# Hybrid decoder layer: the output projection as seven half-size products of sums

## The chip, the cores and the metric

The kernel runs on one core of one Trainium2 chip. The metric is the device time of one execution in microseconds (us). The engines in the text: PE (TensorE, matmul), DVE (VectorE), ACT (ScalarE), POOL (GpSimd), SP (SyncE, which issues most DMAs).

## The reference

One sequence of 512 rows, width 2048. The three mixers give `diff_out` (512x1024), `ssd_out` (512x512) and `xattn_out` (512x512); what follows them is what the change is about:

```python
diff_out = o.reshape(B, S, DIFF_WIDTH) * jax.nn.silu(dg)      # 8 heads of 128 columns
...
mixed = jnp.concatenate([diff_out, ssd_out, xattn_out], axis=-1)
return x + rms_norm(mixed @ w_out, post_norm_w)               # w_out is 2048 x 2048
```

All is float32.

## The kernel before

Every dense product is made of three matmuls (`mm3`, L94 to L97): each operand is split into a high part in the matmul's 32-bit format and a low part, and hi\*hi, hi\*lo and lo\*hi are added up in PSUM. The high part is a copy on ACT (L247 for weights), the low part a subtraction on DVE (`sub_hi`, L100). Weights come in chunks of 128x1024 (512 KB) through `fetch`, which keeps three chunks loaded (`raw`) and two split (`whi`, `wlo`).

In order of time: projections, SSD mixer, cross attention, then the eight heads of differential attention. The gate products `dg` (48 matmuls of 512 columns for each of 8 heads) run beside the last heads' attention: ACT takes the SiLU (L835) and POOL multiplies the head's output with it (L836). Each head's output `do` is normalized by `col_sums` (L154 to L163: squares on ACT, an addition on DVE at L159, a split, one matmul) and `neg2_rstd`. The activations stand transposed: 16 k tiles of 128 feature rows by 512 sequence columns, `do` 0 to 7, then `zs` and `xo` (the tiles that the SSD and the cross attention left).

The output projection splits these 16 k tiles (`mxh`, `mxl`, L851 and L100) and walks `OUT_BLOCKS`: blocks of 512, 512, 512, 256 and 256 output columns, for each 16 k tiles by 4 row tiles by 3 matmuls. The order of the k tiles starts with `zs` and `xo` (`KORDER_OUT`). A block's four PSUM banks are squared on ACT into `ssq` and multiplied with the norm's weights on DVE (`evac_out`, L861 and L863). The last block is done row tile by row tile, so that each row tile's norm, residual addition (L891) and store run while PE works on the next.

A scheduler with a model of time sets the order on each engine within what the code and the buffers allow; each engine then works strictly in that order.

Of the kernel before, what the change touches and what calls it, by code (L numbers as in the profile page):

```python
# [68 lines left out]
def hymba_kernel(ctx: ExitStack, tc: tile.TileContext, x, mem, positions, pre_norm_w, w_in,  # L69
# [24 lines left out]
    def mm3(ps, ah, al, bh, bl, start, stop):  # L94
        nc.tensor.matmul(ps, ah, bh, start=start, stop=False)  # L95
        nc.tensor.matmul(ps, ah, bl, start=False, stop=False)  # L96
        nc.tensor.matmul(ps, al, bh, start=False, stop=stop)  # L97
# [122 lines left out]
    def split_chunk():  # L220
# [6 lines left out]
        if i >= len(chunks) - 4:  # L227
            j = i - (len(chunks) - 4)
            his, los = [], []
            for e in range(2):  # L230
                hi = ft(slots_p, [P, 2, 256], f"s{KORDER_OUT[4 * j + e]}", f"lwh{j}{e}", dt=F32R)
                lo = ft(slots_p, [P, 2, 256], f"s{KORDER_OUT[4 * j + 2 + e]}", f"lwl{j}{e}",
                        dt=F32R)
                rv = raw[:, e * 512:(e + 1) * 512].rearrange("p (k c) -> p k c", k=2)
                nc.scalar.activation(hi, rv, AF.Copy)
                sub_hi(lo, rv, hi)
                his += [hi[:, 0], hi[:, 1]]
                los += [lo[:, 0], lo[:, 1]]
            pieces[i] = (his, los)
            return  # L240
        else:
            hi = ft(wpool, [P, CHUNK], "whi", f"whi{i}", dt=F32R)
            lo = ft(wpool, [P, CHUNK], "wlo", f"wlo{i}", dt=F32R)
# [490 lines left out]


# [85 lines left out]
    for p in range(4):  # L821
# [7 lines left out]
        for i in range(2):  # L829
            head(2 * p + i, q[i], k[i], v_pair[p])  # L830
    for p in range(4):
        for i in range(2):
            ps = dense_ws(hT, S, f"dg{p}{i}")
            gt = ft(ap, [P, S], "raw", f"dgate{p}{i}", 2)
            nc.scalar.activation(gt, ps, AF.Silu)  # L835
            nc.gpsimd.tensor_tensor(do[2 * p + i], do[2 * p + i], gt, ALU.mult)  # L836
        exp_table()
# [91 lines left out]
```

## Time and profile before

| what | value |
|---|---|
| median of 3 runs | 918.95 us (918.36 to 919.58) |
| the profiled execution, its own time | 918.23 us |
| its span in the trace | 916.5 us |
| granted PE clock, mean | 0.995 |
| busy shares PE / DVE / ACT / POOL | 98% / 57% / 46% / 13% |
| output projection, first to last `wo` matmul | 728.05 to 907.67 us |

The span is the time from the first to the last recorded instruction; the execution's own time is 1.73 us longer. A share is busy time over the span. Times in the text below that have two decimals are positions in this span or durations of single instructions.

### The profile page before, as it was taken

To read this page: it belongs to the slowest core of one execution; us is meant where nothing else is said; L and a number is where in the kernel's file an instruction comes from. 1 tells how busy PE (TensorE), PEld (TensorE's weight loads), DVE (VectorE), ACT (ScalarE), POOL (GpSimd) and SP (SyncE) were. 2 spreads that over 40 slices of the span, in tenths; PEclk is the share of its full clock that TensorE was granted. 3 is DMA by queue.
4 is the path that set the end of the run, shared out by engine and by line. 5 is a ranking of instruction groups with operands and counts; after the bars stand their busy time and mean duration, and the time that the engine had idled before them with its cause. 6 is when DMAs were issued, how large, how long until landed. Compare 5 with 4: busy or idle time off the path is not lost.

```text
span 916.5 us, 12561 instructions
## 1 busy us (share of the span) xinstructions
PE 898.5 (98%) x4794; PEld 767.4 (84%) x4794; DVE 519.7 (57%) x974; ACT 425.2 (46%) x705; POOL 123.4 (13%) x134
## 2 busy tenths in 40 slices
PE   7899999999999999999999999999999999999996
PEld 6799888888888888898899889888788878888896
DVE  5674545595575432485867678586755653232336
ACT  4653344455356642344554455454676733231331
POOL 2320000006000113320240122114111010000000
PEclk9999999999999999999999999999999999999998
DMA  6963332354352333442433343333233262322228
GB/s 224 351 165 85 85 84 69 91 149 115 93 133 74 93 93 104 115 104 73 112 95 89 93 109 81 99 93 103 70 92 92 69 241 95 102 92 92 93 70 275
DMA packets 137093, 104.42 MB, mean 114 GB/s; under 512 B 8693, under 2 KB 121026, under 8 KB 136394
## 3 DMA queue, kind: packets, MB, share of 16 engines
q1 hardware_dynamic: 136010, 103.11, 39.4%
q8 instruction: 37, 0.61, 0.3%
q0 software_dynamic: 1024, 0.53, 0.2%
...
## 4 chain that ended last, share of the span: by engine, by line
PE 90%; DMA 3%; ACT 2%; DVE 2%; SPq 1%; POOL 1%; issue 1%; DVEq 0%; POOLq 0%; ACTq 0%
PE wo L96 6%; PE wo L97 6%; PE wo L95 6%; PE v L97 3%; PE v L95 3%; PE v L96 3%; PE q L95 3%; PE q L96 3%; PE q L97 3%; PE xbc L96 3%; PE xbc L97 3%; PE xbc L95 3%; PE k L96 3%; PE k L95 3%; PE k L97 3%; PE dg L96 2%
## 5 line engine op out<-in xcount | busy, mean ns | idle before, releaser
L100 DVE TENSOR_TENSOR wlo<-raw,whi 128x1024 fp32r<-128x1024 f32 (+2 forms) x149 | 188.3, 1264 | 215.2 <-ACT whi L247 202.1
L247 ACT ACTIVATE whi<-raw 128x1024 fp32r<-128x1024 f32 (+1 forms) x132 | 139.7, 1059 | 210.4 <-PE wo L97 89.0
L96 PE MATMUL wo<-wlo,mxh 128*128 128x512 f32 (+1 forms) x256 | 93.3, 365 | 0.0
L97 PE MATMUL wo<-whi,mxl 128*128 128x512 f32 (+1 forms) x256 | 93.1, 364 | 0.0
L95 PE MATMUL wo<-whi,mxh 128*128 128x512 f32 (+1 forms) x256 | 81.8, 366 | 0.9 <-ACT dgate L835 0.9
L97 PE MATMUL v<-whi,hTl 128*128 128x256 f32 (+1 forms) x256 | 72.9, 286 | 0.0
L96 PE MATMUL v<-wlo,hTh 128*128 128x256 f32 (+1 forms) x256 | 72.8, 285 | 0.0
L95 PE MATMUL v<-whi,hTh 128*128 128x256 f32 (+1 forms) x256 | 72.5, 285 | 0.0
L792 ACT ACTIVATE p<-sc,nm 128x128 f32<-128x128 f32 (+3 forms) x64 | 33.3, 524 | 63.1 <-DVE nm L788 57.7
L95 PEld LDWEIGHTS wo<-whi,mxh 128*128 128x128 f32 x256 | 48.0, 188 | 9.8 <-ACT dgate L835 1.4
L96 PEld LDWEIGHTS wo<-wlo,mxh 128*128 128x128 f32 x256 | 48.2, 188 | 8.3
L97 PEld LDWEIGHTS wo<-whi,mxl 128*128 128x128 f32 x256 | 48.2, 188 | 8.0
L96 PE MATMUL k<-hTl,whi 128*128 128x512 f32 x128 | 50.9, 397 | 0.0
L97 PE MATMUL xbc<-hTh,wlo 128*128 128x512 f32 x128 | 50.7, 396 | 0.0
L95 PE MATMUL q<-hTh,whi 128*128 128x512 f32 x128 | 50.7, 396 | 0.0
L97 PE MATMUL dg<-hTh,wlo 128*128 128x512 f32 x128 | 50.7, 396 | 0.0
L96 PE MATMUL dg<-hTl,whi 128*128 128x512 f32 x128 | 50.6, 396 | 0.0
L96 PE MATMUL xbc<-hTl,whi 128*128 128x512 f32 x128 | 50.6, 395 | 0.0
L95 PE MATMUL dg<-hTh,whi 128*128 128x512 f32 x128 | 50.6, 395 | 0.0
L97 PE MATMUL k<-hTh,wlo 128*128 128x512 f32 x128 | 50.5, 395 | 0.0
L96 PE MATMUL q<-hTl,whi 128*128 128x512 f32 x128 | 50.4, 394 | 0.0
L97 PE MATMUL q<-hTh,wlo 128*128 128x512 f32 x128 | 50.4, 394 | 0.0
...
## 6 DMA issues: line engine op xcount, KB each, us to landing
...
```

What stands on the lines that cost most here:

```text
L95: nc.tensor.matmul(ps, ah, bh, start=start, stop=False)
L96: nc.tensor.matmul(ps, ah, bl, start=False, stop=False)
L97: nc.tensor.matmul(ps, al, bh, start=False, stop=stop)
L100: nc.vector.tensor_tensor(lo, src, hi.bitcast(F32), ALU.subtract)
L247: nc.scalar.activation(hi[:, :n], raw[:, :n], AF.Copy)
L792: nc.scalar.activation(pc[c][:, :w], sc[c][:, :w], AF.Exp, bias=nm[:, c:c + 1], scale=DSC, accum_out=ls[:, c:c + 1])
```

## The change

The output projection is done as Strassen's scheme in Winograd's form, one level deep. The 2048 inputs are halved in k (tiles `zs`, `xo` against tiles `do`), the 512 rows of a weight group's output in halves of 256, and the 2048 output columns go in four groups of 512, each halved into 256. Instead of eight block products of a group there are seven, each between a weight block or a sum of weight blocks (`U1` to `U4`) and an activation block or a sum of activation blocks (`N1`, `N2`, `T3`, `T4`). A product is four units of k; a unit is 12 matmuls of 128x256, so a group has 28 units and the projection 1,344 matmuls where there were 576 of 512 columns and 384 of 256.

- Weight blocks are loaded as 128x1024 tiles. In groups 0 to 2 POOL forms `U1` and `U3` (two additions of 128x1024 each, L957) and DVE `U2` and `U4`; in the last group DVE forms `U3`, POOL the others.
- Each unit's weights are split 512 columns at a time (`owh` on ACT, `owl` on DVE), three units ahead of the unit that is issued, in four buffers.
- Activation sums are formed in place on DVE (`sums_c`, 16 instructions of 256; `comb_d`, 8) and split (`cA`, `cB`, `cC`, 8 each of 512; `cD`, 8 of 256).
- The products are recombined on DVE (`T`, one operand in PSUM), squared on ACT and multiplied with the norm's weights on POOL in groups 0 to 2, on DVE in the last (`finish`).
- The SiLU of a gate is written back to PSUM, and the gate's multiplication is on DVE instead of POOL.
- The last two products of the last group run in row halves; the rows' norm, residual addition (now 8 instructions of 256 for each row tile) and store follow.

The diff, cut:

```diff
-    mixed = [None] * KT
-    for kt in KORDER_OUT:
-        src = (do + zs + xo)[kt]
-        mh = ft(big, [P, 512], "big", f"mxh{kt}", dt=F32R)
-        ml = ft(big, [P, 512], "big", f"mxl{kt}", dt=F32R)
-        nc.scalar.activation(mh, src, AF.Copy)
-        sub_hi(ml, src, mh)
-        mixed[kt] = (mh, ml)
...
-    tags = (("d", "d", "d", "tr"), ("sc", "sc", "sc", "av"))
-    for c in range(4):
-        col0, ncols = OUT_BLOCKS[c]
-        ps = dense_xs(mixed, [bank(tags[c % 2][t], f"wo{c}_{t}") for t in range(NT)], ncols,
-                      KORDER_OUT)
-        for t in range(NT):
-            evac_out(ps[t], t, c)
...
+    for a in zs + xo:
+        nc.vector.tensor_tensor(a[:, 256:], a[:, :256], a[:, 256:], ALU.subtract)
...
+            last_po = head(2 * p + i, q[i], k[i], v_pair[p])
+            if 2 * p + i < 7:
+                head_norm(2 * p + i, last_po, ap, "osq", "ory", "p1")
...
+    def gate_head(h, after=None):
+        ps = dense_ws(hT, S, f"dg{h}", after)
+        nc.scalar.activation(ps, ps, AF.Silu)
+        nc.vector.tensor_tensor(do[h], do[h], ps, ALU.mult)
...
+    def split_sum(j, kind, src, names):
+        hi = half_tile(f"c{kind}h{j}")
+        lo = half_tile(f"c{kind}l{j}")
+        nc.scalar.activation(hi, src, AF.Copy)
+        sub_hi(lo, src, hi)
+        for nm, cs in zip(names, (lsum, rsum)):
+            comb[j][nm] = (hi[:, cs], lo[:, cs])
...
+    def sums_c(j):
+
+        a, b = src1[j], do[j]
+        for cs, other in ((rsum, b[:, rsum]), (lsum, a[:, rsum])):
+            nc.vector.scalar_tensor_tensor(a[:, cs], other, -1.0, a[:, cs], ALU.mult,
+                                           ALU.subtract)
...
+    def comb_d(j):
+
+        a, b = src1[j], do[j]
+        nc.vector.scalar_tensor_tensor(b[:, lsum], a[:, rsum], -1.0, b[:, lsum],
+                                       ALU.mult, ALU.subtract)
+        both = half_tile(f"cD{j}")
+        nc.scalar.activation(both[:, lsum], b[:, lsum], AF.Copy)
+        sub_hi(both[:, rsum], b[:, lsum], both[:, lsum])
+        comb[j]["T4"] = (both[:, lsum], both[:, rsum])
...
+    plans = {(3, 0): [(comb_a, 4), (comb_a, 5)], (3, 1): [(comb_a, 6)], (4, 0): [(comb_a, 7)],
+             (6, 0): [(sums_c, 0), (sums_c, 1), (sums_c, 2), (comb_c, 0)],
+             (6, 1): [(sums_c, 3), (sums_c, 4), (comb_c, 1)],
+             (7, 0): [(sums_c, 5), (comb_c, 2)], (7, 1): [(sums_c, 6), (comb_c, 3)]}
+    head_norm(7, last_po, ep, "pw", "pw", "osp", 2, [(comb_a, j) for j in range(4)])
...
+    PROD = {1: ("A11", "B11"), 2: ("A12", "B21"), 3: ("U4", "B22"), 4: ("A22", "T4"),
+            5: ("U1", "N1"), 6: ("U2", "N2"), 7: ("U3", "T3")}
+    NG = D // 512
+    ORDER = [(1, 5, 7, 6, 2, 4, 3)] * (NG - 1) + [(1, 7, 6, 2, 4, 5, 3)]
+    seq = [(g, q, u) for g in range(NG) for q in ORDER[g] for u in range(4)]
...
+    def combine(g, eng, dst, a, b, at):
+        for u in range(2):
+            w = wt[g]
+            eng.tensor_tensor(w[at, u], w[a, u], w[b, u], ALU.add)
+            w[dst, u] = w[at, u]
+
+    def start_group(g):
+
+        if g == 0:
+            for nm in ("A11", "A21"):
+                load_block(0, nm)
+        load_block(g, "A22")
+        for u in range(2):
+            wt[g]["U1", u] = raw_tile(f"oU1_{g}{u}")
...
+        combine(g, nc.gpsimd, "U1", "A21", "A22", "U1")
+        if g < NG - 1:
+            combine(g, nc.gpsimd, "U3", "A11", "A21", "A21")
...
+        if g < NG - 1:
+            if q == 5:
+                combine(g, nc.vector, "U2", "U1", "A11", "U1")
+                load_block(g, "A12")
+            if q == 7:
+                load_block(g + 1, "A11")
+            if q == 6:
+                combine(g, nc.vector, "U4", "U2", "A12", "U1")
+            if q == 4:
+                load_block(g + 1, "A21")
+            if q == 3:
+                start_group(g + 1)
+            return
+        if q == 1:
+            combine(g, nc.vector, "U3", "A11", "A21", "A11")
+            combine(g, nc.gpsimd, "U2", "U3", "A22", "A21")
+        if q == 7:
+            load_block(g, "A12")
+        if q == 6:
+            combine(g, nc.gpsimd, "U4", "U2", "A12", "A21")
...
+    def split_product(n):
+        if n >= len(seq):
+            return
+        g, q, u = seq[n]
+        src = wt[g][PROD[q][0], u // 2][:, 512 * (u % 2):512 * (u % 2) + 512]
+        if n < len(seq) - 8:
+            hi, lo = (ft(ep, [P, 512], f"ow{x}", f"ow{x}{n}", 4, F32R) for x in "hl")
...
+        nc.scalar.activation(hi, src, AF.Copy)
+        sub_hi(lo, src, hi)
+        split[n] = [[t[:, 256 * k:256 * k + 256] for k in range(2)] for t in (hi, lo)]
...
+    def finish(g, r, c, ts=(0, 1)):
+        o = acc(g, r, c)
+        jk = ft(ep, [P, 256], "jk", f"jk{g}{r}{c}{ts[0]}", 2, BF16)
+        for t in ts:
+            nc.scalar.activation(jk, o[:, t], AF.Square, scale=1.0 / math.sqrt(D),
+                                 accum_out=ssq[:, 2 * c + t, 2 * g + r:2 * g + r + 1])
+        w = pws[g][:, r].unsqueeze(1).broadcast_to([P, len(ts), 256])
+        tt = slice(ts[0], ts[-1] + 1)
+        (nc.gpsimd if g < NG - 1 else nc.vector).tensor_tensor(o[:, tt], o[:, tt], w, ALU.mult)
...
+        for g in range(NG):
+            for r in range(2):
+                xs = xr[t, g // 2][:, (g % 2) * 512 + r * 256:(g % 2) * 512 + r * 256 + 256]
+                nc.vector.scalar_tensor_tensor(xs, oacc[g, r, t // 2][:, t % 2], y, xs,
+                                               ALU.mult, ALU.add)
...
+    def product(n, ps, ts=(0, 1)):
+        hi, lo = split[n]
+        g, q, u = seq[n]
+        for t in ts:
+            tsl = slice(t * P, (t + 1) * P)
+            for kk in range(2):
+                bh, bl = comb[2 * u + kk][PROD[q][1]]
+                last = mm3(ps[:, t], bh[:, tsl], bl[:, tsl], hi[kk], lo[kk],
+                    u == 0 and kk == 0 and t == ts[0], u == 3 and kk == 1 and t == ts[-1])
+        return last
...
+    rest = {2: [(comb_c, 4)], 3: [(comb_c, 5)], 4: [(comb_c, 6)], 5: [(comb_c, 7)],
+            6: [(comb_b, 0)], 7: [(comb_b, 1)], 8: [(comb_b, 2)], 9: [(comb_b, 3)],
+            10: [(comb_b, 4)], 11: [(comb_b, 5)], 12: [(comb_b, 6)], 13: [(comb_b, 7)],
+            14: [(comb_d, 0), (comb_d, 1)], 15: [(comb_d, 2), (comb_d, 3)],
+            16: [(comb_d, 4), (comb_d, 5)], 17: [(comb_d, 6), (comb_d, 7)]}
...
+        if q == 6 and g < NG - 1:
+            T(acc(g, 1, 1), acc(g, 0, 0), ps)
+            T(acc(g, 1, 0), acc(g, 1, 1), qps[g, 7])
+        elif q == 6:
+            T(acc(g, 0, 1), acc(g, 0, 0), ps)
+            T(acc(g, 1, 1), acc(g, 0, 1), qps[g, 7])
+        if q == 2:
+            if g < NG - 1:
+                T(acc(g, 0, 1), acc(g, 1, 1), qps[g, 5])
+                T(acc(g, 1, 1), acc(g, 1, 0), qps[g, 5])
+                finish(g, 1, 1)
+            T(acc(g, 0, 0), acc(g, 0, 0), ps)
+            finish(g, 0, 0)
+        if q == 4:
+            T(acc(g, 1, 0), acc(g, 1, int(g == NG - 1)), ps)
+            finish(g, 1, 0)
+        if q == 3:
+            T(acc(g, 0, 1), acc(g, 0, 1), ps)
+            finish(g, 0, 1)
...
+    for t in (0, 1):
+        load_rows(t)
+        write_rows(t)
+    g = NG - 1
+    N = len(seq)
+    for t in (0, 1):
+        load_rows(2 + t)
+        for q, n in ((5, N - 8), (3, N - 4)):
+            ps = qps2[q] if t else qps[g, q]
+            with tc.issue_after(last.ins):
+              for u in range(4):
+                last = product(n + u, ps, (t,))
+            for r in range(2):
+                if q == 5 or r == 0:
+                    T(acc(g, r, 1)[:, t], acc(g, r, 1)[:, t], ps[:, t])
+            finish(g, int(q == 5), 1, (t,))
+        write_rows(2 + t)
```

On DVE, at the end of the last head's attention (L159 is the addition in head 7's norm; `mxl` the splits of k tiles, `wlo` of weight chunks), before:

```order
L159 TENSOR_TENSOR osq_6214<-osq_6214,oup_6217 64x512
L100 TENSOR_TENSOR wlo_6687<-raw_6650,whi_6686 128x1024
L100 TENSOR_TENSOR mxl_6758<-z_2544,mxh_6757 128x512
L100 TENSOR_TENSOR osp_6218<-osq_6214,osp_6218 64x512
L100 TENSOR_TENSOR mxl_6762<-z_2607,mxh_6761 128x512
L100 TENSOR_TENSOR mxl_6766<-z_2698,mxh_6765 128x512
L100 TENSOR_TENSOR mxl_6770<-z_2761,mxh_6769 128x512
L100 TENSOR_TENSOR mxl_6774<-xo_1297,mxh_6773 128x512
L100 TENSOR_TENSOR wlo_6717<-raw_6684,whi_6716 128x1024
```

The same place in the change; `cAl` and `cCl` are splits of activation blocks, `owl` of a unit's weights, L868 is `sums_c`:

```order
L159 TENSOR_TENSOR osq_6357<-osq_6357,oup_6360 64x512
L100 TENSOR_TENSOR cAl_6369<-z_2544,cAh_6368 128x512
L100 TENSOR_TENSOR cAl_6373<-z_2607,cAh_6372 128x512
L868 SCALAR_TENSOR_TENSOR z_2544<-do_3605,z_2544 128x256
L100 TENSOR_TENSOR osp_6361<-osq_6357,osp_6361 64x512
L868 SCALAR_TENSOR_TENSOR z_2607<-do_3749,z_2607 128x256
L100 TENSOR_TENSOR owl_6829<-oA_00_6810,owh_6828 128x512
L868 SCALAR_TENSOR_TENSOR z_2544<-z_2544 128x256
L100 TENSOR_TENSOR owl_6833<-oA_00_6810,owh_6832 128x512
L868 SCALAR_TENSOR_TENSOR z_2607<-z_2607 128x256
L100 TENSOR_TENSOR owl_6837<-oA_01_6812,owh_6836 128x512
L100 TENSOR_TENSOR owl_6841<-oA_01_6812,owh_6840 128x512
```

The last two weight splits of the gates, which stood behind L159, stand before it, and all splits and sums that group 0 needs stand behind it: from there to the last `owl` of group 0 there are 64 instructions of 512 columns (28 `owl`, 8 each of `cA`, `cB`, `cC`, 5 recombinations, 7 of head 7's norm and gate), 24 scalar_tensor_tensors of 256 (16 `sums_c`, 8 `comb_d`), 8 `cD` splits and 4 multiplications of `pw` of 256, and 4 additions of 1024. On PE, 38 gate matmuls of 512 stand between head 7's last attention matmul and the first of group 0.

On POOL, from the first weight sum on, in the change (`oU`, `oA` are weight tiles of 1024; before, eight L836 multiplications and the one of `pw` stood here, and nothing behind them):

```order
L957 TENSOR_TENSOR oU_00_6822<-oA_00_6814,oA_00_6818 128x1024
L957 TENSOR_TENSOR oU_01_6823<-oA_01_6816,oA_01_6820 128x1024
L957 TENSOR_TENSOR oA_00_6814<-oA_00_6810,oA_00_6814 128x1024
L957 TENSOR_TENSOR oA_01_6816<-oA_01_6812,oA_01_6816 128x1024
L957 TENSOR_TENSOR oU_10_7361<-oA_10_7283,oA_10_7357 128x1024
L1032 TENSOR_TENSOR oacc_7182<-oacc_7182,pw_6913 128x512
L1032 TENSOR_TENSOR oacc_6917<-oacc_6917,pw_6913 128x512
L957 TENSOR_TENSOR oA_10_7283<-oA_10_7010,oA_10_7283 128x1024
```

POOL's work now goes on through the projection: four sums each for groups 0 to 2, six for the last, and four products with `pw` of 512 for each of the groups 0 to 2.

At the end of the program on DVE, before (the last row tile; `wo_3` is its last PSUM bank):

```order
L863 TENSOR_TENSOR oacc_6824<-wo_3_8079,pw 128x256
L885 TENSOR_REDUCE oss_8131<-ssq 128x1
L291 TENSOR_TENSOR ort_8134<-ors_8133 128x1
L292 SCALAR_TENSOR_TENSOR ort_8134<-oss_8131,ort_8134 128x1
L293 SCALAR_TENSOR_TENSOR ors_8133<-ort_8134,ors_8133 128x1
L891 SCALAR_TENSOR_TENSOR oacc_6824<-oacc_6824,ors_8133,xr_8077 128x256
L891 SCALAR_TENSOR_TENSOR oacc_6824<-oacc_6824,ors_8133,xr_8077 128x512 x3
L891 SCALAR_TENSOR_TENSOR oacc_6824<-oacc_6824,ors_8133,xr_8077 128x256
```

And in the change, from the last product's recombination (`oq33b`, behind the last matmul) on:

```order
L1098 TENSOR_TENSOR oacc_8668<-oacc_8668,oq33b 128x256
L272 TENSOR_TENSOR ort_8947<-ors_8946 128x1
L273 SCALAR_TENSOR_TENSOR ort_8947<-oss_8944,ort_8947 128x1
L1032 TENSOR_TENSOR oacc_8670<-oacc_8670,pw_8526 128x256
L274 SCALAR_TENSOR_TENSOR ors_8946<-ort_8947,ors_8946 128x1
L1032 TENSOR_TENSOR oacc_8668<-oacc_8668,pw_8526 128x256
L1043 TENSOR_REDUCE oss_9024<-ssq 128x1
L1050 SCALAR_TENSOR_TENSOR xr_8883<-oacc_7267,ors_8946,xr_8883 128x256
L1050 SCALAR_TENSOR_TENSOR xr_8883<-oacc_7182,ors_8946,xr_8883 128x256
L1050 SCALAR_TENSOR_TENSOR xr_8883<-oacc_7780,ors_8946,xr_8883 128x256
L1050 SCALAR_TENSOR_TENSOR xr_8883<-oacc_7711,ors_8946,xr_8883 128x256
L1050 SCALAR_TENSOR_TENSOR xr_8885<-oacc_8293,ors_8946,xr_8885 128x256
```

The eight residual additions of row tile 2 (L1050, with `ors_8946`) stand behind the last recombination and before row tile 3's own norm and its eight additions, which follow these rows. The 16 of row tiles 0 and 1 stand earlier.

## Rows read from the trace of the kernel before

**Rows 1.** The page: busy time and share of each engine; the chain that ended last.
```profile
PE 898.5 (98%) x4794; PEld 767.4 (84%) x4794; DVE 519.7 (57%) x974; ACT 425.2 (46%) x705; POOL 123.4 (13%) x134
...
PE 90%; DMA 3%; ACT 2%; DVE 2%; SPq 1%; POOL 1%; issue 1%; DVEq 0%; POOLq 0%; ACTq 0%
```

**Rows 2.** Windows: length, busy us per engine, granted PE clock, DMA share, GB/s.
```profile
core 0: us, PE busy (x) PEld busy (x) DVE busy (x) ACT busy (x) POOL busy (x), PEclk, DMA share, GB/s
...
728.00:862.00 134.00, 133.06 (x578) 107.97 (x577) 45.30 (x47) 41.40 (x58) 3.22 (x2) 1.00 0.35 121
862.00:907.50 45.50, 45.50 (x385) 45.46 (x383) 23.41 (x48) 12.92 (x35) 0.00 (x0) 1.00 0.42 131
907.50:916.50 9.00, 0.17 (x2) 0.00 (x0) 3.83 (x10) 0.97 (x4) 0.00 (x0) 0.71 0.73 275
```

**Rows 3.** Timeline of PE in the output projection: start, busy, operation.
```profile
728.05 0.84 PE L95 MATMUL wo<-whi,mxh 128*128 128x512 f32 x3
...
734.10 0.50 PE L95 MATMUL wo<-whi,mxh 128*128 128x512 f32 x1 [0.94 <-ACT dgate L835]
...
862.00 0.63 PE L95 MATMUL wo<-whi,mxh 128*128 128x256 f32 x4
...
907.39 0.28 PE L97 MATMUL wo<-lwh,mxl 128*128 128x256 f32 x1
```

**Rows 4.** Timeline of DVE at 732 us, back to back.
```profile
731.99 0.68 DVE L100 TENSOR_TENSOR mxl<-do,mxh 128x512 fp32r<-128x512 f32 x1
732.59 0.68 DVE L293 SCALAR_TENSOR_TENSOR ory<-osq,ory 128x512 f32<-128x512 f32 x1
733.19 1.22 DVE L100 TENSOR_TENSOR wlo<-raw,whi 128x1024 fp32r<-128x1024 f32 x1
734.32 0.75 DVE L818 SCALAR_TENSOR_TENSOR do<-do,subc,ory 128x512 f32<-128x512 f32 x1
```

**Rows 5.** Timeline of DVE, residual additions; the group of its 256-wide subtractions.
```profile
904.63 2.46 DVE L891 SCALAR_TENSOR_TENSOR oacc<-oacc,ors,xr 128x512 f32<-128x512 f32 x4
...
L100 DVE TENSOR_TENSOR vl<-v,vh 128x256 fp32r<-128x256 f32 x16 | 6.6, 419 | 1.3 <-ACT vh L428 1.3
```

**Rows 6.** Timeline of POOL at three places.
```profile
387.38 2.28 POOL L751 TENSOR_TENSOR sw_k<-sw_k,sinT 128x512 f32<-128x512 f32 x1
...
620.03 1.29 POOL L751 TENSOR_TENSOR sw_k<-sw_k,sinT 128x512 f32<-128x512 f32 x1
...
668.95 1.29 POOL L836 TENSOR_TENSOR do<-do,dgate 128x512 f32<-128x512 f32 x1 [10.60 <-ACT dgate L835]
```

**Rows 7.** Timeline of DVE at the same three places.
```profile
386.34 2.17 DVE L100 TENSOR_TENSOR wlo<-raw,whi 128x1024 fp32r<-128x1024 f32 x1 [3.55 <-ACT whi L247]
...
620.14 2.26 DVE L100 TENSOR_TENSOR wlo<-raw,whi 128x1024 fp32r<-128x1024 f32 x1 [1.95 <-ACT whi L247]
...
669.40 0.69 DVE L100 TENSOR_TENSOR aTl<-atr,aTh 128x512 fp32r<-128x512 f32 x1 [1.17 <-ACT aTh L803]
```

**Rows 8.** POOL's groups by shape: count, busy us, mean ns, idle before.
```profile
L836 POOL TENSOR_TENSOR do<-do,dgate 128x512 f32<-128x512 f32 x8 | 10.3, 1290 | 88.0 <-ACT dgate L835 74.2 <-DVE do L818 13.8
L629 POOL TENSOR_TENSOR conv<-conv,E 128x384 f32<-128x384 f32 x4 | 4.0, 1012 | 54.6 <-DVE E L628 43.0 <-DVE conv L622 11.6
```

**Rows 9.** Timelines of PE and DVE behind the last head's attention.
```profile
715.20 0.28 PE L97 MATMUL av<-aTh,vl 128*128 128x128 f32 x1
...
717.22 0.68 DVE L159 TENSOR_TENSOR osq<-osq,oup 64x512 f32<-64x512 f32 x1 [5.68 <-ACT oup L158]
```

**Rows 10.** Timelines of ACT and DVE behind the last matmul.
```profile
907.70 0.38 ACT L861 ACTIVATE jk<-wo 128x256 bf16<-128x256 f32 x1 [4.09 <-PE wo L97]
...
910.01 2.87 DVE L891 SCALAR_TENSOR_TENSOR oacc<-oacc,ors,xr 128x256 f32<-128x256 f32 x5 [0.17 <-DMA xr<-in_x_dram]
```

**Rows 11.** Timeline of ACT: copies of 512 columns back to back.
```profile
720.98 1.66 ACT L851 ACTIVATE mxh<-z 128x512 fp32r<-128x512 f32 x3
```

**Rows 12.** Windows early in the run, columns as in Rows 2.
```profile
0.00:10.00 10.00, 5.40 (x18) 4.18 (x19) 2.89 (x7) 3.60 (x6) 3.27 (x16) 1.00 0.73 231
20.00:30.00 10.00, 7.47 (x25) 5.13 (x24) 4.08 (x11) 7.33 (x12) 2.09 (x2) 0.86 0.85 319
```

More of the change, by code (lines that the diff above doesn't have):

```diff
@@ L96, in mm3 @@
         nc.tensor.matmul(ps, ah, bl, start=False, stop=False)
[L97 removed]
+        return nc.tensor.matmul(ps, al, bh, start=False, stop=stop)
     def sub_hi(lo, src, hi):
@@ L226, in split_chunk @@
         n = nkt * n1
[L227 to L243, printed above, removed]
+        hi = ft(wpool, [P, CHUNK], "whi", f"whi{i}", dt=F32R)
+        lo = ft(wpool, [P, CHUNK], "wlo", f"wlo{i}", dt=F32R)
         if i < N_POOL:
@@ L263, in dense_ws @@
             hi, lo = fetch()
+            if after:
+                after(ch)
             for kk in range(8):
@@ L829, in hymba_kernel @@
         for i in range(2):
[L830 to L837, printed above, removed]
+            last_po = head(2 * p + i, q[i], k[i], v_pair[p])
[5 more added lines that the diff above has]
+        nc.vector.tensor_tensor(do[h], do[h], ps, ALU.mult)
+    EARLY = 2
+    for h in range(EARLY):
+        gate_head(h)
     for _ in range(3):
@@ new lines, in hymba_kernel, with load_pw @@
+    for h in range(EARLY, 8):
+        gate_head(h, run_plan(h))
+    sums_c(7)
+    exp_table()
+    pws = {}
+    def load_pw(g):
+        pws[g] = ft(ep, [P, 2, 256], "pw", f"pw{g}", 2)
+        nc.sync.dma_start(pws[g].rearrange("p r c -> p (r c)"),
+                          post_norm_w[0, 512 * g:512 * g + 512].partition_broadcast(P))
+        for r in range(2):
+            nc.vector.tensor_scalar(pws[g][:, r], pws[g][:, r], (-0.5, 0.5)[r], None, ALU.mult)
+    ssq = const.tile([P, NT, 8], F32, name="ssq")
@@ new lines, in hymba_kernel, with raw_tile @@
+    PROD = {1: ("A11", "B11"), 2: ("A12", "B21"), 3: ("U4", "B22"), 4: ("A22", "T4"),
[3 more added lines that the diff above has]
+    seq = [(g, q, u) for g in range(NG) for q in ORDER[g] for u in range(4)]
+    wt = [{} for _ in range(NG)]
+    split = {}
+    nraw = [0]
+    def raw_tile(name):
+        nraw[0] += 1
+        at = (nraw[0] - 1) % 8
+        if at == 0:
+            return ft(ep, [P, 1024], "raw2", name, 1)
+        tag, bufs = (("raw", 3), ("whi", 2), ("wlo", 2))[(0, 0, 0, 1, 2, 1, 2)[at - 1]]
+        return ft(wpool, [P, CHUNK], tag, name, bufs)[:, :1024]
@@ L884, in hymba_kernel, with load_rows, write_rows @@
+    xr = {}
+    def load_rows(t):
+        for h in range(2):
+            xr[t, h] = raw_tile(f"xr{t}{h}")
+            nc.sync.dma_start(xr[t, h], x2[t * P:(t + 1) * P, h * 1024:(h + 1) * 1024])
+    def write_rows(t):
         ss = ft(small, [P, 1], "ss", f"oss{t}")
@@ new lines, in product @@
+    def product(n, ps, ts=(0, 1)):
+        hi, lo = split[n]
+        g, q, u = seq[n]
+        for t in ts:
[5 more added lines that the diff above has]
+        return last
+    V = nc.vector
+    start_group(0)
+    AHEAD = 3
+    for n in range(AHEAD):
+        split_product(n)
```

134 lines of the change are left out of this document (94 added, 40 removed).

## The prediction

> **What bounds the kernel now.** The page comes first: PE is busy 98% of the span and carries 90% of the chain that ended last, DVE is busy 57%, ACT 46%, POOL 13% [rows 1]. So matmul columns are what the time is made of. Those are averages, and the change touches one stage, so the second view is the windows of the output projection [rows 2]: from 728 to 907.5 us PE is busy 178.6 of 179.5 us at a granted clock of 1.00, DVE 68.7, ACT 54.3, POOL 3.2. PE has no slack there; DVE has 110 us of it, and POOL stands nearly still. The third view is PE's timeline in that stage [rows 3]. It gives the price of a matmul by starts: 576 of 512 columns between 728.05 and 862.00, less one idle gap of 0.94 us, are 0.231 us each; 383 of 256 columns between 862.00 and 907.39 are 0.1185 us each. Half the columns cost half the time, so cutting matmuls to 256 wide loses nothing by itself. Behind the last matmul (907.67) 8.8 us pass until the span ends at 916.5: PE works 0.17 us in that window [rows 2].
>
> **What the change should give PE.** 1,344 matmuls of 256 by 0.1185 us are 159.3 us; before, the stage took 907.67 less 728.05, 179.6 us. If PE were fed, 20.3 us would be gained. A unit is 12 matmuls, 1.42 us; a group of 28 units is 39.8 us. So the questions are whether DVE and POOL can feed units at that pace, and what the end costs.
>
> **DVE's prices.** Back to back, a DVE instruction of 512 columns starts 0.60 us after the one before it (731.99 to 732.59 to 733.19), one of 1024 takes 1.13 us (733.19 to 734.32) [rows 4]. A scalar_tensor_tensor of 256 is the difference of five such instructions (2.87 us, two of them of 256 and three of 512, [rows 10]) and four (2.46 us, [rows 5]): 0.41 us. A subtraction of 256 shows 0.42 us of its own [rows 5]; less the 0.08 us by which instructions in a row overlap (0.68 against 0.60) that is 0.34 us, which I take for the multiplications of `pw` too.
>
> **POOL's price, and what it does to DVE.** Before, POOL does no 1024-wide addition. Its 384-wide one takes 1.012 us, its 512-wide 1.290 us [rows 8]: 0.278 us for 128 columns, so 1.29 and four steps more are 2.40 us for 1024. The bounds are one of 512, 1.29, and two of them, 2.58. The Trainium skill, "GPSIMD Engine Reference", section 3.1 (elementwise, side by side), measures 4497 ns for an addition twice as long; half of that, an estimate, is 2.25 us, and the four additions of group 0 below would cost 0.6 us less by it.
>
> What matters more is that DVE and POOL stop each other. At 386.34 a 1024-wide subtraction on DVE takes 2.17 us instead of 1.22, and POOL's 512-wide product that begins at 387.38 takes 2.28 instead of 1.29; at 620.14 DVE's takes 2.26 beside one of POOL's of 1.29 [rows 6, 7]. The lengths fit one working at a time: at 620 POOL's first ends at 621.32, and 1.08 us more are DVE's own. At 669.40 DVE reads PSUM with one operand and takes 0.69 us, its own time, beside a POOL product that began at 668.95 [rows 6, 7]. So DVE's splits and sums, both operands in SBUF, wait out each POOL instruction; recombinations, with one operand in PSUM, don't. The upper bound of what a POOL instruction costs DVE is then its whole length; the lower is nothing, where DVE waits for something else anyway.
>
> **Group 0.** All activation sums and splits and the 28 weight splits of the group stand behind the L159 of head 7's norm. That instruction began 1.74 us after the end of head 7's last attention matmul (715.48 to 717.22, [rows 9]). In the change 38 gate matmuls of 0.231 us, 8.8 us, lie between that matmul and the first of group 0, so DVE starts its list 7.0 us ahead of the projection. The list: 64 of 512 by 0.60, 38.4 us; 24 of 256 by 0.41, 9.8; 12 by 0.34, 4.1; 4 of 1024 by 1.13, 4.5; together 56.8 us. POOL's four additions, 9.6 us, fall into the same stretch, for their tiles take the buffers that the last gate chunks leave; by the row at 620 I count them in full: 66.4 us. The last split is ready 59.4 us after the first matmul and group 0 ends one unit later, at 60.8, where PE alone would need 39.8. **That is 21 us of PE waiting for DVE, as much as the whole saving.** ACT is no bound there: its copies of 512 are 0.52 us (1.66 for three, [rows 11]), some 60 of them 31 us.
>
> **Groups 1 to 3.** PE needs 3 by 39.75, 119.3 us. DVE needs per group 35 to 36 of 512, 4 of 1024 and 2 of 256, 26.2 and 26.8 us, and POOL's four sums and four products (1.29 each) 14.8; summed, 41.0 and 41.6 against 39.75. In group 3 the splits of the last eight units stand early, so that 21.5 us of DVE and 19.6 of POOL (six sums, four products left from group 2), 41.1 us, must fit before unit 20, 28.4 us of PE. If every POOL instruction stops DVE, the excess is 1.3, 1.8 and 12.7, in all 15.8 us; the four split buffers lend 5.7 us (four units) against it. Bounds 0 and 15.8; I take 6, a little over half of the 10.1 left, since in these groups DVE also waits for buffers, and POOL's time then costs nothing.
>
> **The end.** Before, 2.34 us lie between the last matmul and the first residual addition (907.67 to 910.01), then 2.87 us of additions, then 3.6 us until the last store has landed [rows 10, 2]. In the change there is one more multiplication on the way (0.42, as the other 256-wide ones), and row tile 2's eight additions stand in DVE's queue between the last recombination and row tile 3's norm, whose own eight follow: 16 by 0.41, 6.6 us. 2.34 + 0.42 + 6.6 + 3.6 = 12.9. If row tile 2's eight were through in time it would be 9.7; at the 0.49 us that the busy time of one gives (0.41 and 0.08) 14.2.
>
> **What costs nothing.** The gates' multiplications move from POOL to DVE (8 by 0.60, one operand in PSUM), the first eight differences of 256 lie in cross attention: together some 8 us in stages where PE is busy and DVE, 57% over the span, is not; if that cover were gone, 8 us. The weights' DMA traffic is as before, at a DMA share of 0.35 to 0.42 [rows 2].
>
> **The sum.** 728.05 + 60.8 + 119.3 + 6 + 12.9 = 927.05 of span; with the 1.73 us that the profiled execution took beyond its span, **928.7 us**, against 918.23 for that execution and 918.95 for the median: 1.1% slower. What this kernel can tell from no change is about 0.2%, 1.8 us. Around it 922 to 935 for the likeliest case alone.
>
> **The rivals.**
> - *The saving and the bill cancel.* DVE pays in group 0 as above, but nothing stalls later and row tile 2's additions are through in time: 728.05 + 60.8 + 119.3 + 9.7 + 1.73 = 919.6. For it speaks that DVE waits for buffers in groups 1 and 2; against it group 3, whose list is longest. 0.09.
> - *The other side: POOL's sums cost DVE nothing.* If they fall where DVE waits for ACT's copies or a load, group 0 ends at 51.2 and later groups don't stall: 728.05 + 51.2 + 119.3 + 12.9 + 1.73 = 913.2, faster by 0.6%. It decides from the point where 11.6 of my 15.6 us of POOL's cost are gone (917.1). For it: POOL begins as soon as its tiles have landed, and DVE and ACT hand over to each other in small steps. Against it: DVE's own 56.8 us stand against 46.8 us (7.0 and 39.8) in which they would have to be done, so its list has hardly a gap to give. 0.16.
> - *Everything stalls.* All 15.8 us, and an end of 14.2: 939.9. 0.15.
> - *The clock.* In group 0 PE would be busy about two thirds. From 20 to 30 us, 75% busy, the granted clock was 0.86, though 1.00 in the first 10 us, 54% busy [rows 12]; at 907.5, with PE still, it is 0.71 over the window [rows 2]. The forecast keeps 1.00, by the first 10 us. If it fell to the lower level, 1.2 of 2.4 GHz, through group 0, a unit would take 2.84 us and the group 79.5 instead of 60.8: 947.4. The Trainium skill, "TensorE: Matmul & The Clock Gate", section "What's actually happening", says that the slow level is the default and activity releases it, which speaks for this rival. The trace agrees with it only in part, with 0.71 and 0.86 beside that 1.00. 0.07.
>
> That leaves 0.53 for the forecast. **Chances**: slower 0.53 + 0.15 + 0.07 = 0.75, the same 0.09, faster 0.16. The range: below 914 lies half of the faster case (0.08), above 938 the clock's (0.07) and part of the full stall (0.05), so 914 to 938 holds 8 in 10.
>
> **What the changed profile would show.** If right: in the first group (some 60 us from the first `oq` matmul) PE is busy two thirds, its idle time released by DVE's L100 of `owl` and the `c` tiles; DVE is near 100% there, with 512-wide splits of 3 us beside POOL's L957 of 2.4; the next groups take 40 to 44 us; the end behind the last matmul takes 13 us, with 16 L1050 in a row. Wrong, if the first group takes 40 to 50 us, if DVE shows idle gaps that ACT or a load ends while POOL works, if splits beside L957 keep their 0.6 us, or if row tile 2's additions lie before the last matmul.

## The result, and the profile after

The changed kernel takes 943.34 us (median of 4 runs, 942.87 to 944.16) against 919.03 for the kernel before: a ratio of 1.0266, 95% interval 1.0248 to 1.0284, slower by 2.7%. The forecast was 928.7 us, range 914 to 938: the direction was right, but 24.3 us were lost where 9.8 were forecast. The profiled execution took 943.54 us with a span of 941.8.

The page's first rows: busy time by engine, and the chain that ended last.

```profile
PE 893.7 (95%) x5178; PEld 780.5 (83%) x5178; DVE 638.9 (68%) x1157; ACT 466.3 (50%) x821; POOL 185.5 (20%) x155
...
PE 81%; DVE 10%; DMA 3%; issue 3%; POOL 1%; ACT 1%; SPq 0%; DVEq 0%; POOLq 0%; ACTq 0%
```

Beside [rows 1], PE gave up 9 points of the chain and DVE took 8. Where that is shows in windows, one for each of the four groups and one for the end (length, busy us per engine, granted clock, DMA share, GB/s):

```profile
729.38:789.27 59.89, 47.16 (x339) 44.83 (x338) 55.93 (x95) 33.02 (x66) 16.17 (x5) 0.89 0.24 75
789.27:835.96 46.69, 42.52 (x338) 41.43 (x337) 41.37 (x41) 22.11 (x50) 23.35 (x12) 0.96 0.33 102
835.96:880.44 44.48, 40.96 (x338) 39.94 (x337) 37.71 (x42) 21.59 (x45) 17.46 (x9) 1.00 0.31 101
880.44:929.50 49.06, 41.97 (x338) 40.22 (x336) 43.83 (x67) 19.84 (x46) 17.66 (x7) 1.00 0.41 138
929.50:941.80 12.30, 0.00 (x0) 0.00 (x0) 8.98 (x29) 1.90 (x8) 0.00 (x0) 0.64 0.56 220
```

Against the forecast's terms: the projection starts at 729.38 instead of 728.05 (1.3 us late), group 0 takes 59.9 us (forecast 60.8), groups 1 to 3 take 140.2 (forecast 119.3 and 6 of stalls), the end 12.3 (forecast 12.9). 1.3 − 0.9 + 14.9 − 0.6 are 14.7 us; 928.7 with them is 943.4, against the 943.5 of the profiled execution (the rest is rounding). One term is far off, that of groups 1 to 3: 20.9 us above PE's 119.3, where 6 were taken. PE's idle time ahead of the projection is 8.26 us before and after, so the late start is more busy time on PE, not a wait; which work it is was not looked into.

Group 0 is near the forecast in its length and in the engine that sets it. DVE's timeline, from head 7's norm to the last weight split of the group (start, busy; in brackets the idle time before an instruction and what ended it):

```profile
722.45 0.69 DVE L159 TENSOR_TENSOR osq<-osq,oup 64x512 f32<-64x512 f32 x1 [3.19 <-ACT oup L158]
...
733.13 0.41 DVE L868 SCALAR_TENSOR_TENSOR xo<-do,xo 128x256 f32<-128x256 f32 x1
733.46 0.41 DVE L868 SCALAR_TENSOR_TENSOR z<-z 128x256 f32<-128x256 f32 x1
733.80 0.68 DVE L100 TENSOR_TENSOR cAl<-xo,cAh 128x512 fp32r<-128x512 f32 x1
...
737.71 2.18 DVE L100 TENSOR_TENSOR owl<-oU,owh 128x512 fp32r<-128x512 f32 x1 [2.89 <-ACT owh L1011]
739.81 2.60 DVE L868 SCALAR_TENSOR_TENSOR z<-z 128x256 f32<-128x256 f32 x1
742.33 2.56 DVE L868 SCALAR_TENSOR_TENSOR xo<-xo 128x256 f32<-128x256 f32 x1
...
786.50 0.69 DVE L100 TENSOR_TENSOR owl<-oU,owh 128x512 fp32r<-128x512 f32 x1
```

The list runs from 722.45 to 787.19, where the group's 28th `owl` ends: 64.7 us; the forecast had 66.4. POOL's four sums cost DVE 2.9 us of waiting for the first one and 5.8 us in three held instructions, 8.7 of the 9.6 counted. The 24 scalar_tensor_tensors of 256 start 0.34 us apart where nothing holds them (733.13, 733.46, 733.80); the forecast took 0.41, which made the list 1.7 us too long.

PE did not wait for that last weight split, though. Its last gap in the group ends with an activation split, and the group ends 2.1 us behind the 28th `owl`, where the forecast had one unit, 1.4:

```profile
776.69 0.38 PE L97 MATMUL oq<-owh,cBl 128*128 128x256 f32 x1 [0.56 <-DVE cBl L100]
```

The end is as forecast: the eight additions of row tile 2 and those of row tile 3 stand behind the last matmul (929.5), one after the other.

```profile
931.62 3.25 DVE L1050 SCALAR_TENSOR_TENSOR xr<-oacc,ors,xr 128x256 f32<-128x256 f32 x8
...
935.36 3.26 DVE L1050 SCALAR_TENSOR_TENSOR xr<-oacc,ors,xr 128x256 f32<-128x256 f32 x8
```

Now the term that was off. DVE and POOL at the start of group 1:

```profile
790.08 3.46 DVE L100 TENSOR_TENSOR owl<-oA,owh 128x512 fp32r<-128x512 f32 x2
793.46 4.56 DVE L100 TENSOR_TENSOR owl<-oU,owh 128x512 fp32r<-128x512 f32 x2
798.06 3.28 DVE L957 TENSOR_TENSOR oU<-oU,oA 128x1024 f32<-128x1024 f32 x1
801.26 3.44 DVE L100 TENSOR_TENSOR owl<-oU,owh 128x512 fp32r<-128x512 f32 x2
804.63 2.85 DVE L100 TENSOR_TENSOR owl<-oA,owh 128x512 fp32r<-128x512 f32 x1
807.40 1.21 DVE L957 TENSOR_TENSOR oU<-oU,oA 128x1024 f32<-128x1024 f32 x1
```

```profile
788.25 3.02 POOL L957 TENSOR_TENSOR oU<-oA,oA 128x1024 f32<-128x1024 f32 x1 [43.64 <-DMA oA<-in_w_out_dram]
791.24 3.45 POOL L1032 TENSOR_TENSOR oacc<-oacc,pw 128x512 f32<-128x512 f32 x2
794.65 2.82 POOL L957 TENSOR_TENSOR oA<-oA,oA 128x1024 f32<-128x1024 f32 x1
797.44 2.82 POOL L957 TENSOR_TENSOR oU<-oA,oA 128x1024 f32<-128x1024 f32 x1
800.22 3.94 POOL L1032 TENSOR_TENSOR oacc<-oacc,pw 128x512 f32<-128x512 f32 x2
804.12 2.81 POOL L957 TENSOR_TENSOR oA<-oA,oA 128x1024 f32<-128x1024 f32 x1
```

POOL works through eight instructions without a gap from 788.25 to 806.93; such a stretch is called a burst below (the expectations say run). From 790.08 to 807.40 DVE gets eight done, one for each of POOL's; alone they would take 5.3 us (seven of 0.60, one of 1.13, [rows 4]). PE, which uses a split every 1.42 us, runs dry. The first and the last of its gaps that belong to a burst, in each of the groups 1 to 3:

```profile
798.08 0.38 PE L96 MATMUL oq<-owl,cAh 128*128 128x256 f32 x1 [1.09 <-DVE owl L100]
...
803.07 0.49 PE L96 MATMUL oq<-owl,cAh 128*128 128x256 f32 x1 [1.72 <-DVE owl L100]
...
839.28 0.39 PE L96 MATMUL oq<-owl,cAh 128*128 128x256 f32 x1 [0.17 <-DVE owl L100]
...
849.42 0.39 PE L96 MATMUL oq<-owl,cAh 128*128 128x256 f32 x1 [1.14 <-DVE owl L100]
...
885.92 0.39 PE L96 MATMUL oq<-owl,cAh 128*128 128x256 f32 x1 [2.32 <-DVE owl L100]
...
894.34 0.39 PE L96 MATMUL oq<-owl,cCh 128*128 128x256 f32 x1 [1.10 <-DVE owl L100]
```

POOL works from 788 to 807, from 833 to 848 and from 878 to 894 us, so these gaps lie in its bursts or within 2 us behind them. There are 13 gaps in the three groups, 14.6 us in all; DVE's `owl` ends 12 of them, and only two, 1.3 us together, lie elsewhere. The other 6.3 of the 20.9 us stand in PE's busy time (125.5 us against 119.3). A part of that is the clock: behind three gaps in group 1 the granted clock is 0.53 from 803 to 806 us. How much it cost there was not measured.

Behind the burst DVE has time, but can't use it; who waited for whom from 789 to 917.9 us (us in all, times, longest):

```profile
DVE owl L100 <- ACT owh L1011: 12.0, 22, 1.0
...
ACT owh L1011 <- PE oq L97: 38.9, 46, 2.3
```

DVE waits for the high part, and that for PE to free one of the four split buffers.

### The profile page after: what moved, and what is told of

It reads as the page before. It is cut to its first block, busy times and chain, and to the rows that moved or that the text cites. A ratio compares the mean times of both kernels' runs of the same rounds, so it can differ in the third digit from the quotient of the medians.

```text
span 941.8 us, 13732 instructions
## 1 busy us (share of the span) xinstructions
PE 893.7 (95%) x5178; PEld 780.5 (83%) x5178; DVE 638.9 (68%) x1157; ACT 466.3 (50%) x821; POOL 185.5 (20%) x155
## 3 DMA queue, kind: packets, MB, share of 16 engines
q0 software_dynamic: 1024, 0.53, 0.2%
## 4 chain that ended last, share of the span: by engine, by line
PE 81%; DVE 10%; DMA 3%; issue 3%; POOL 1%; ACT 1%; SPq 0%; DVEq 0%; POOLq 0%; ACTq 0%
PE oq L96 3%; DVE owl L100 3%; PE v L97 3%; PE v L95 3%; PE v L96 3%; PE oq L97 3%; PE q L96 3%; PE q L95 3%; PE q L97 3%; PE xbc L95 3%; PE xbc L96 3%; PE xbc L97 3%; PE oq L95 3%; PE k L96 3%; PE k L95 3%; PE k L97 3%
## 5 line engine op out<-in xcount | busy, mean ns | idle before, releaser
L100 DVE TENSOR_TENSOR wlo<-raw,whi 128x1024 fp32r<-128x1024 f32 (+2 forms) x121 | 150.9, 1247 | 124.4 <-ACT whi L226 110.5
L226 ACT ACTIVATE whi<-raw 128x1024 fp32r<-128x1024 f32 (+1 forms) x104 | 110.1, 1059 | 125.5 <-issue 29.0
L100 DVE TENSOR_TENSOR owl<-oA,owh 128x512 fp32r<-128x512 f32 x68 | 66.4, 990 | 7.3 <-ACT owh L1011 7.3
L776 ACT ACTIVATE p<-sc,nm 128x128 f32<-128x128 f32 (+3 forms) x64 | 33.4, 525 | 64.6 <-DVE nm L772 59.3
L1011 ACT ACTIVATE owh<-oA 128x512 fp32r<-128x512 f32 x68 | 42.4, 629 | 45.2 <-PE oq L97 34.4
L957 POOL TENSOR_TENSOR oU<-oA,oA 128x1024 f32<-128x1024 f32 x8 | 27.5, 3444 | 141.8 <-PE dg L96 89.8
L95 PE MATMUL k<-hTh,whi 128*128 128x512 f32 x128 | 50.4, 394 | 0.0
L95 PE MATMUL xbc<-hTh,whi 128*128 128x512 f32 x128 | 50.3, 393 | 0.0
L96 PEld LDWEIGHTS v<-wlo,hTh 128*128 128x128 f32 x256 | 48.4, 189 | 0.3
```

The lines of the kernel that those rows point to most:

```text
L100: nc.vector.tensor_tensor(lo, src, hi.bitcast(F32), ALU.subtract)
L226: nc.scalar.activation(hi[:, :n], raw[:, :n], AF.Copy)
L776: nc.scalar.activation(pc[c][:, :w], sc[c][:, :w], AF.Exp, bias=nm[:, c:c + 1], scale=DSC, accum_out=ls[:, c:c + 1])
L957: eng.tensor_tensor(w[at, u], w[a, u], w[b, u], ALU.add)
L1011: nc.scalar.activation(hi, src, AF.Copy)
```

## The experiments

Each ratio is to the kernel before, timed beside the run; its interval follows in brackets. Windows are of the groups 0, 1, 2, 3 in this order.

**All of POOL's work on DVE.**

```diff
-        combine(g, nc.gpsimd, "U1", "A21", "A22", "U1")
+        combine(g, nc.vector, "U1", "A21", "A22", "U1")
...
-        (nc.gpsimd if g < NG - 1 else nc.vector).tensor_tensor(o[:, tt], o[:, tt], w, ALU.mult)
+        nc.vector.tensor_tensor(o[:, tt], o[:, tt], w, ALU.mult)
```

(and the other three `combine` on POOL alike)

> All 18 weight sums and the 12 products with the norm's weights that POOL did in the projection are done by DVE; POOL does nothing there. Theory (POOL's instructions stop DVE in one run of eight at the start of each group, and the three units of lead can't bridge it): DVE's list per group is 26.5 + 4.5 + 2.4 = 33 us against 39.8 of PE, so groups 1 to 3 take 40 to 41 us each instead of 46.7, 44.5 and 49.1, and group 0, whose list is 56.8 + 4.5 us, takes about 56 instead of 59.9: 918 to 923 us. Rival (the waits in groups 1 to 3 are the hand-over from ACT to DVE to PE with a short lead, whoever forms the sums): DVE has 27 us more to do, 943 us or more.

926.04 us, ratio 1.0073 (1.0056 to 1.0091): 17 us less, with more work on DVE.

```profile
729.07:785.00 55.93, 46.57 (x339) 44.46 (x338) 54.42 (x99) 32.82 (x67) 0.00 (x0) 0.91 0.26 81
785.00:826.94 41.94, 40.17 (x337) 39.72 (x336) 37.24 (x53) 22.35 (x48) 0.00 (x0) 1.00 0.37 114
826.94:867.85 40.91, 40.27 (x339) 39.85 (x337) 34.18 (x51) 21.92 (x45) 0.00 (x0) 1.00 0.36 110
867.85:909.64 41.79, 40.84 (x338) 40.02 (x336) 38.53 (x74) 19.73 (x46) 0.00 (x0) 1.00 0.49 163
```

Groups 1 to 3 fall from 140.2 to 124.6 us, group 0 from 59.9 to 55.9. The median is 3 us above the expected range, and 5.3 us above PE's 119.3 stay; the hand-over rival, which needed 943 or more, is out.

**Only the products with the norm's weights on DVE** (the last line of that diff alone).

> Only the 12 products with the norm's weights move from POOL to DVE; the sums stay. Theory (each POOL instruction in the run of eight costs DVE its own length): three runs lose four products of 1.1 us of POOL's own time each, for 0.6 us on DVE outside the run: 930 to 938 us. Rival (hand-over): same or slower, 943 to 947.

944.06 us, 1.0274 (1.0257 to 1.0291): nothing gained; the expectation failed. The time lies in the rival's range, but the run above has ruled out the rival's cause. The moved product joins the queue that POOL's sums hold up, and waits out a sum itself:

```profile
834.03 2.90 DVE L1032 TENSOR_TENSOR oacc<-oacc,pw 128x512 f32<-128x512 f32 x1
```

**Only the sums on DVE** (the other half of the diff).

> Only the 18 sums move to DVE; the 12 products with the norm's weights stay on POOL. It is the other half of the run that moved the products alone and gained nothing. Theory (the sums are the cost, the products of 512 are not): 923 to 929 us, as with both on DVE. Rival (the two only pay together): 933 or more.

924.88 us, 1.0064 (1.0049 to 1.0079), groups 1 to 3 125.7 us. The sums are the whole of what POOL's work cost: with the products moved as well the kernel was no faster (926.04).

**No splits that wait for POOL's sums.**

```diff
-        src = wt[g][PROD[q][0], u // 2][:, 512 * (u % 2):512 * (u % 2) + 512]
+        nm = PROD[q][0]
+        if g < NG - 1 and q in (5, 7):
+            nm = "A22" if q == 5 else "A11"
+        src = wt[g][nm, u // 2][:, 512 * (u % 2):512 * (u % 2) + 512]
```

> POOL forms the same sums at the same size into the same tiles, but in groups 0 to 2 products 5 and 7 split an unsummed block instead (A22 for U1, A11 for U3), so that no split of these products waits for POOL; these products are not the ones that the output needs. It parts two ways in which POOL's sums can cost time: by stopping DVE, or by being late. Theory now (they stop DVE, and late in a group DVE idles because only four split buffers exist): groups 1 and 2 stay at 44 to 47 us each, the first wait of 3.4 us in group 0 goes, 936 to 943 us. Rival (the splits of products 5 and 7 wait for POOL's late sums): groups 1 and 2 take 40 to 42 us, 927 to 933.

948.81 us, 1.0323 (1.0307 to 1.0338), above both ranges. Groups 1 and 2 take 48.7 us each, and in them neither ACT nor DVE waits for POOL's result; all six gaps of PE are ended by DVE's `owl`. DVE, meanwhile, works back to back, and four splits that take 2.5 us alone take three times as long beside POOL:

```profile
794.88 7.36 DVE L100 TENSOR_TENSOR owl<-oA,owh 128x512 fp32r<-128x512 f32 x4
```

So in these groups the sums cost by stopping DVE, not by being late. In group 0, still 59.3 us, the wait did not go but moved: DVE's own sum for U2 now waits 2.28 us for POOL's U1. That the kernel became 5 us slower was not expected; in group 1 both of DVE's own sums for U2 now fall into POOL's burst, where one did, but whether that is the reason was not tested.

**Sums in four pieces.**

```diff
-            eng.tensor_tensor(w[at, u], w[a, u], w[b, u], ALU.add)
+            for i in range(4 if eng is nc.gpsimd else 1):
+                cs = slice(256 * i, 256 * i + 256) if eng is nc.gpsimd else slice(0, 1024)
+                eng.tensor_tensor(w[at, u][:, cs], w[a, u][:, cs], w[b, u][:, cs], ALU.add)
```

> The changed kernel with each of POOL's 18 sums of 128x1024 cut into four of 128x256; the same work stays on POOL. Theory (while POOL has work in a row, DVE gets one instruction in between two of POOL's, so what counts is the length of one POOL instruction): a split in the run waits 0.6 to 0.7 us instead of 2.2, DVE gives a split every 1.3 us where PE wants one every 1.4, and groups 1 to 3 take 41 to 44 us each: 928 to 936 us. Rival (what counts is the time that POOL holds DVE in all, which the cut doesn't lessen): 942 us or more.

946.34 us, 1.0295 (1.0281 to 1.0309): the theory in this form failed, and the time lies in the rival's range; groups 1 to 3 take 142.7 us. DVE's splits do get through faster (two in 1.96 us instead of 3.46), but POOL's second sum for U1 comes behind two products and half of U3, ACT can copy it only at 801.63 (800.29 in the change), and now DVE waits for that copy:

```profile
790.55 1.96 DVE L100 TENSOR_TENSOR owl<-oA,owh 128x512 fp32r<-128x512 f32 x2
...
802.29 2.91 DVE L100 TENSOR_TENSOR owl<-oU,owh 128x512 fp32r<-128x512 f32 x2 [5.81 <-ACT owh L1013]
```

So the length of one POOL instruction isn't what counts alone. That all the time for which POOL holds DVE comes back on one side or the other fits these rows, but is argued.

**Three split buffers instead of four.**

```diff
-            hi, lo = (ft(ep, [P, 512], f"ow{x}", f"ow{x}{n}", 4, F32R) for x in "hl")
+            hi, lo = (ft(ep, [P, 512], f"ow{x}", f"ow{x}{n}", 3, F32R) for x in "hl")
...
-    AHEAD = 3
+    AHEAD = 2
```

> The changed kernel with three split buffers instead of four, and splits two units ahead instead of three. Theory (POOL's sums stop DVE in one run per group, and only the lead of the split buffers, 1.4 us a unit, bridges it; DVE can't save up the idle time that it has later in the group): each of groups 1 to 3 loses 1 to 1.5 us more, 946 to 949 us. Rival (DVE's and POOL's work in a group, added up, is what a group takes): no change, 942 to 944.5.

951.74 us, 1.0356 (1.0341 to 1.0371): 8.4 us more, above the range; groups 61.9, 48.6, 45.2 and 52.0 us. The work of DVE and POOL in a group is the same as in the change, so it is not its sum that sets the time: the rival is out. The theory's sizes were not right either: groups 1 to 3 lost 2.0, 0.7 and 3.0 us, and group 0 lost 2.0, which it had not. More buffers were not tried, nor the same sums spread over the group.

**Group 0: the list.** The sums for T3 and N2 and their splits left out.

```diff
     def sums_c(j):
-
+        return
         a, b = src1[j], do[j]
...
-        split_sum(j, "C", src1[j], ("T3", "N2"))
+        ntile[0] += 2
+        comb[j]["T3"], comb[j]["N2"] = comb[j]["B11"], comb[j]["N1"]
```

> Leaves out the sums for the activation blocks T3 and N2 and their splits (products 7 and 6 use the blocks of products 1 and 5 instead, so these two products are not the ones that the output needs): 16 scalar_tensor_tensors of 256 and 8 splits of 512 less on DVE, 11.4 us, all in group 0's list; PE does as many matmuls. Theory (group 0 ends when DVE's list ends): group 0 about 48 to 50 us instead of 59.9, the kernel 931 to 935 us. Rival (POOL's late first sum and the lower clock set group 0's length, not the list): 939 to 944.

933.71 us, 1.0163 (1.0148 to 1.0179), group 0 50.9 us: 9.0 us less for 11.4 us of list (10.2 us by the 0.34 measured above).

**Group 0: the clock.**

```diff
+    FILL = {4: 16, 5: 6, 6: 16}
...
+        if n in FILL:
+            fill = bank("sc", f"fill{n}")
+            for _ in range(FILL[n]):
+                nc.tensor.matmul(fill, hA[0][:, :P], hA[0], start=True, stop=True)
```

> Adds 38 matmuls of 512 columns into a bank that nobody reads, at the places of group 0 where PE stood idle (before product 5 and before its third unit), 8.8 us of PE where 7.7 us were idle, so that the granted clock stays up. Theory (DVE's list ends group 0, so the lower clock was hidden behind it): granted clock near 1.00 in group 0, the group still 59 to 62 us, the kernel 942 to 946. Rival (the lower clock cost its own 5 to 7 us): 935 to 939.

943.96 us, 1.0271 (1.0256 to 1.0286). Group 0's clock rises from 0.89 to 0.97 and the group still takes 60.7 us. The same 10 us in the change and in this run:

```profile
738.00:748.00 10.00, 5.67 (x24) 5.01 (x24) 10.00 (x10) 4.65 (x9) 6.61 (x3) 0.52 0.01 2
...
738.00:748.00 10.00, 5.86 (x29) 4.97 (x30) 10.00 (x10) 4.72 (x10) 6.48 (x3) 0.85 0.01 2
```

The clock was 0.52 without the filling matmuls and 0.85 with them, and DVE was busy 10.00 of 10 us in both.

**Group 0 the plain way, all sums on DVE.** Eight block products, so that group 0 needs no sums; those of groups 1 to 3 are formed beside it (N1 as −N2 − B22, into the tiles of B12).

```diff
-    ORDER = [(1, 5, 7, 6, 2, 4, 3)] * (NG - 1) + [(1, 7, 6, 2, 4, 5, 3)]
+    ORDER = [(10, 11, 12, 13)] + [(1, 5, 7, 6, 2, 4, 3)] * (NG - 2) + [(1, 7, 6, 2, 4, 5, 3)]
...
+                    bh, bl = comb[2 * u + kk][("B11", "B12", "B21", "B22")[2 * k + c]]
+                    last = mm3(dps[r, c][:, t], bh[:, tsl], bl[:, tsl], hi[kk], lo[kk],
...
```

> All sums and products with the norm's weights on DVE, as in the run before that did this, and group 0 done in the plain way (eight block products, 384 matmuls of 256, splits of the unsummed blocks; the sums for groups 1 to 3 are formed beside it). Theory (group 0 is bound by DVE's list, which has to bring all activation sums and splits ahead of its matmuls): PE needs 45.5 us there, DVE's list of 48.5 us starts 7 us ahead, so group 0 takes 46 to 50 us instead of 55.9, the rest as in the run with all on DVE (124.6 and 12.4 us): 914 to 919 us. Rival (the plain group waits as long, since its second half needs splits that stand late in the list): 921 to 926.

916.11 us, 0.9971 (0.9960 to 0.9981): 0.3% faster than before. Group 0 takes 51.4 us, 1.4 above the expected range, of which 3.48 are one wait for ACT's `cBh`; groups 1 and 2 take 39.7 us each, PE's own time.

**The same with POOL's sums in pieces of 256** (`combine` on POOL as in the cut above).

> The kernel with the plain group 0, and POOL forms its sums again, in pieces of 128x256. Theory (short POOL instructions cost DVE little, and DVE is free of 4.5 us per group): the stalls at the start of groups 1 to 3 shrink, 1 to 5 us less than the kernel with all sums on DVE: 911 to 917 us. Rival (any POOL instruction costs DVE its length): 3 to 8 us more than that kernel.

923.77 us, 1.0055 (1.0041 to 1.0068): 7.7 us more than with the sums on DVE, the rival's upper end.

**The plain group with its lower blocks split first.**

```diff
+        rest[i] = [(comb_b, 2 * i), (comb_b, 2 * i + 1)]
+        rest[4 + i] = [(comb_c, 4 + i)]
```

(the last eight units' splits take the `ow` and `cmc` buffers, so that `big` is filled in this order)

> The kernel with the plain group 0 and all sums on DVE, with one change: the splits of the lower blocks (cB) come ahead of the sums for the later groups, which the plain group's second half waited 3.5 us for. Theory (that wait is on the path): group 0 takes 46 to 48 us instead of 51.4: 910 to 914 us. Rival (the wait moves to the cC and N1 splits that group 1 needs): 915 to 919.

910.03 us, 0.9899 (0.9882 to 0.9915), 1.0% faster than the kernel before. Group 0, 1 and the end:

```profile
729.29:774.95 45.66, 45.66 (x388) 45.62 (x387) 43.45 (x92) 26.10 (x60) 0.00 (x0) 1.00 0.32 102
774.95:814.25 39.30, 39.30 (x335) 39.30 (x334) 31.98 (x46) 21.52 (x45) 0.00 (x0) 1.00 0.37 115
...
895.95:908.40 12.45, 0.00 (x0) 0.00 (x0) 9.07 (x30) 1.90 (x8) 0.00 (x0) 0.71 0.57 220
```

PE has no idle time in the first two. Group 3, not shown, takes 42.0 us with one gap of 1.6 us. The end is as long as in the change.

**Its end without row tile 0's additions** (`if t > 0:` ahead of the scalar_tensor_tensor in `write_rows`).

> The fastest version so far, without the eight residual additions of row tile 0 (its rows are stored as the bare residual). Theory (DVE's queue is too long in the last products, so that row tile 2's eight additions fall behind the last matmul): the end behind the last matmul shrinks from 12.4 us by 2.5 to 3.3 us, 906.5 to 907.7. Rival (the end is the chain of the last row tile and the last store): 909.5 to 910.5.

910.07 us, 0.9904 (0.9887 to 0.9920): no change; the expectation failed, and the time lies in the rival's range. Row tile 2's additions now begin 0.4 us before the last matmul ends (896.2), but the order, planned anew, has the last recombination behind them:

```profile
895.81 3.26 DVE L1068 SCALAR_TENSOR_TENSOR xr<-oacc,ors,xr 128x256 f32<-128x256 f32 x8
898.99 0.42 DVE L1153 TENSOR_TENSOR oacc<-oacc,oq33b 128x256 f32<-128x256 f32 x1
```

So whether the end can be had in 9.7 us stays open; it was not settled by this run.

## Why the prediction was right in sign and wrong in size

- **What PE would gain** (20.3 us if fed): the price is right. In the fastest version groups 1 and 2 take 39.3 and 39.7 us at a clock of 1.00, against the forecast's 39.8. The whole 20.3 us were reached by no version: that one does group 0 the plain way, in 45.7 us, and group 3 in 42.0.
- **Group 0 is DVE's list**: right, by the list's length (64.7 us against 66.4), by DVE's busy time in the group (55.9 of 59.9 us) and by the run with a shorter list. That the group's time came within 0.9 us is in part luck: the sums of 256 were priced 1.7 us too high, and PE ended the group 0.7 us later behind the last weight split than forecast, a split for which it did not wait.
- **POOL's price, and that it stops DVE**: right in kind. The rows give 2.8 us for a sum in the burst; if 0.6 of it are the DVE instruction that was let pass, 2.2 are its own (an estimate), against the forecast's 2.40. The estimate from the Trainium skill, "GPSIMD Engine Reference", section 3.1, was 2.25, nearer to that.
- **The step that failed: "Groups 1 to 3", where DVE's and POOL's times were added up per group, set against 39.75 us, bounded at 15.8 and taken as 6.** The sum per group is not the measure. POOL's sums come in one burst around the start of a group, and during it DVE falls behind PE by more than the four split buffers hold; later in the group DVE is free but can't work ahead (12.0 us of waiting in 22 waits). So 20.9 us were lost where the excess over the group gave at most 15.8. That POOL's sums are the cause is shown by moving them alone to DVE (14.5 of the 20.9 us back, though DVE then has more to do) and by moving the products alone (nothing back). That they act by stopping DVE is shown, for groups 1 and 2, by the run in which neither ACT nor DVE waits for them there, and that the sum per group is not the measure by the further loss with one buffer less. That the burst as such is to blame is read from where PE's gaps lie; no version spread the same sums over the group.
- **The clock rival** came true in its first half (granted 0.52 from 738 to 748 us, near the lower level of 1.2 GHz) and cost nothing in group 0, since DVE's list set the group's time in both cases. In group 1, where the clock fell for 3 us, its cost is open.
- **The other side's rival** (POOL's sums cost DVE nothing) was wrong: without them on POOL the kernel is 18.5 us faster, of 24.3 lost. *Everything stalls* came nearest, but its bound of 15.8 us was passed, and its end of 14.2 us did not come.
- **The end**: 12.3 us against 12.9, in the order forecast.
- The projection's start, 1.3 us late, was not in the sum; PE waited no longer ahead of it, and what more it did was not looked into.
